# Moving part of the last split row of a ReLU row sum to ScalarE, and cutting that row's loads anew

## The chip, the cores and the metric

The kernel runs on one core of one Trainium2 chip. The metric is the device time of one execution in microseconds (us); medians over several executions are quoted. The span of a profile runs from the first to the last instruction that it shows, and in the profiles of this study the time was 1.34 to 1.35 us longer than the span. Three parts of the core matter: ScalarE (ACT in the profile), VectorE (DVE) and the sixteen DMA engines; in the page all loads and stores go through one queue (q1, 2304 packets, 67.18 MB), and SyncE (SP) issues them.

## The reference, cut to what matters

```python
x = randn(32, 512, 1024).astype(float32)          # 67 MB
out = np.sum(np.maximum(x, 0), axis=-1)           # 32 x 512 sums
```

There are 16384 rows of 1024 columns: 128 partitions with 128 rows each. Every input byte is read once, and the arithmetic is one clamp and one sum.

## The kernel before: the parts that the change and the argument touch

All loads go through one queue. Large loads of 16 rows per partition come first, then loads of 8 and 4 rows. This is the end of the stream (cuts marked, some arguments put in words):

```python
PIECES = [360, 260, 404]
...
    def act_row(ap, m, loaded):          # ScalarE: clamp and sum in one ACTIVATE
        i = nc.scalar.activation(out=ap, in_=ap, func=RELU, accum_out=res[:, m : m + 1])
        ...
    def dve_row(ap, accum_out, loaded):  # VectorE: the same in one tensor_scalar
        ...
    first = PIECES[0]
    loaded = load(..., two rows and the first 360 columns of the third)
    act_row(buf[:, c, :], m, loaded)
    dve_row(buf[:, c + 1, :], res[:, m + 1 : m + 2], loaded)
    last_loaded = load(buf[:, c + 3, :], ...)            # the last row
    ... loads of 260 and 404 columns of the third row, into tiles of their own
    act_row(buf[:, c + 3, :], m + 3, last_loaded)
    ... two stores of finished sums
    dve_row(buf[:, c + 2, :first], last[:, w : w + 1], None)                   # 360
    for i in range(1, extra):
        dve_row(parts[i - 1][:, :], last[:, w + i : w + i + 1], arrived[i - 1])  # 260
    nc.vector.wait_ge(sems.dve, n_dve)
    nc.vector.tensor_scalar(out=last[:, :], in0=last[:, :], ..., op0=MAX, op1=ADD,
        accum_out=res[:, NT - 2 : NT - 1]).wait_op(arrived[-1], 16, "sem-ge")   # 404 + 2
    store(NT - 2, 2, n_act, n_dve)
```

The third of these rows is the "split row". Its partial sums are written into extra columns behind the last piece, so the last instruction adds them up with the 404 columns. It therefore waits for VectorE's own semaphore (the partial sums) and for the last load. The final store waits for both engines.

## Time and profile before

| | value |
|---|---|
| time, median of the first 3 executions | 161.29 us |
| profiled execution | 161.02 us, span 159.67 us |
| bytes read | 67.11 MB, 421 GB/s over the span |
| VectorE, ScalarE busy | 74%, 65% of the span |

These are the occupancy lines of the page. The digits are tenths of busy time in 40 slices of 4 us, and the first two rows are VectorE and ScalarE:

```profile
DVE  0000000009999499994999999999999999999986
ACT  3000059990799708996099941999339992499985
DMA  8996996996996998979969969969969969898994
```

VectorE has nothing to do for the first 35 us, and is then busy nearly all the time to the end. The DMA row is high throughout: the packets of q1 took 98.0% of the span of sixteen engines. The last slice, the only one that the change touches, is read in the prediction from the chain of waits and the timeline. In those views L140 is line 140 of the kernel (`dve_row`), L130, or L132 after the change, is `act_row`, and L219 or L226 is the last instruction. TENSOR_SCALAR_CACHE_REDUCE is VectorE's clamp and sum, ACTIVATE is ScalarE's, and behind each stands a READ_ACCUMULATOR instruction of one column (128x1; in the trace of before 188 ns on ScalarE, 82 ns on VectorE). DVEq is an instruction of VectorE's queue, here a wait for a semaphore, and "issue" is time in which the engine waited for nothing that the profile shows.

### The profile page before, as it was taken

The page shows a single profiled execution, that of the slowest core. Times are in us where ns is not written, and L with a number is a line of the kernel's source. Part 1 is how long each engine was busy: PE and PEld are TensorE (multiplying, and loading weights), DVE is VectorE, ACT ScalarE, POOL GpSimd, SP SyncE. Part 2 cuts the span into 40 slices and gives each one's busy share as a digit, 9 for nine tenths or more (in the row PEclk, how much of TensorE's full clock was granted, in tenths as well). Part 3 has the DMA queues.
Part 4 walks back from the last instruction along what each step waited for, and adds up shares of the span by engine and source line. Part 5 has one row for each costly group of instructions (what it writes and reads, how often), then busy time and mean ns, then how long its engine had stood idle before and what let it go on. Part 6 is the DMA issues. An engine that isn't in the chain of part 4 may idle for free.

```text
span 159.7 us, 118 instructions
## 1 busy us (share of the span) xinstructions
DVE 117.5 (74%) x41; ACT 104.2 (65%) x50; POOL 0.2 (0%) x4
## 2 busy tenths in 40 slices
DVE  0000000009999499994999999999999999999986
ACT  3000059990799708996099941999339992499985
POOL 0000000000000000000000000000000000000000
DMA  8996996996996998979969969969969969898994
GB/s 279 509 525 263 525 525 263 525 525 263 525 493 296 525 410 378 525 345 443 525 263 525 525 263 525 525 263 525 525 263 525 525 263 525 345 443 386 409 408 126
DMA packets 2305, 67.18 MB, mean 421 GB/s; under 512 B 641, under 2 KB 897, under 8 KB 1025
## 3 DMA queue, kind: packets, MB, share of 16 engines
q1 hardware_dynamic: 2304, 67.18, 98.0%
q14 instruction: 1, 0.00, 0.0%
HBM read 67.11 MB, written 0.07 MB: 421 GB/s over the span
## 4 chain that ended last, share of the span: by engine, by line
DMA 43%; DVE 34%; ACT 17%; another core or an unknown queue 3%; SPq 1%; issue 0%; DVEq 0%
DMA io<-in_x_dram 43%; DVE res L123 32%; ACT io L115 17%; DVE io L140 1%; SPq L97 1%; DVE piece L219 0%; DVE piece L140 0%; DVEq L218 0%
## 5 line engine op out<-in xcount | busy, mean ns | idle before, releaser
L123 DVE TENSOR_REDUCE res<-io 128x8 f32<-128x8192 f32 (+2 forms) x9 | 101.1, 11287 | 39.9 <-ACT io L115 39.9
L115 ACT ACTIVATE io<-io 128x8192 f32<-128x8192 f32 (+2 forms) x9 | 81.7, 9110 | 47.6 <-DMA io<-in_x_dram 47.6
L130 ACT ACTIVATE io<-io 128x1024 f32<-128x1024 f32 x20 | 20.9, 1045 | 5.9 <-DMA io<-in_x_dram 5.7
L140 DVE TENSOR_SCALAR_CACHE_REDUCE io<-io 128x1024 f32<-128x1024 f32 (+1 forms) x14 | 15.5, 1165 | 0.7 <-DMA io<-in_x_dram 0.6
L130 ACT ACTIVATION_READ_ACCUMULATOR io<-io 128x1 f32 x20 | 3.8, 188 | 0.0
L115 ACT ACT_TABLE_LOAD x1 | 1.3, 1283 | 0.1
L140 DVE DVE_READ_ACCUMULATOR io<-io 128x1 f32 x14 | 1.1, 82 | 0.0
L219 DVE TENSOR_SCALAR_CACHE_REDUCE piece<-piece 128x406 f32<-128x406 f32 x1 | 0.6, 576 | 0.1
L140 DVE TENSOR_SCALAR_CACHE_REDUCE piece<-piece 128x260 f32<-128x260 f32 x1 | 0.4, 424 | 0.0
L264 POOL MEMSET const-bfloat16-1.0<- 128x1 bf16 x1 | 0.1, 101 | 0.0
L264 POOL MEMSET const-uint8-127<- 128x1 uint8 x1 | 0.1, 101 | 0.0
L264 POOL MEMSET const-float32-0.0<- 128x1 f32 x1 | 0.1, 98 | 0.2 <-issue 0.2
L264 POOL MEMSET const-float32-1.0<- 128x1 f32 x1 | 0.1, 98 | 0.0
L140 DVE DVE_READ_ACCUMULATOR piece<-piece 128x1 f32 x1 | 0.1, 83 | 0.0
L219 DVE DVE_READ_ACCUMULATOR piece<-piece 128x1 f32 x1 | 0.1, 83 | 0.0
## 6 DMA issues: line engine op xcount, KB each, us to landing
io<-in_x_dram SPq DMA_DIRECT2D x1, 4096.0 KB, 21.6
io<-in_x_dram SPq DMA_DIRECT2D x1, 2048.0 KB, 26.1
io<-in_x_dram SPq DMA_DIRECT2D x1, 1204.0 KB, 28.6
io<-in_x_dram SPq DMA_DIRECT2D x1, 512.0 KB, 29.4
piece<-in_x_dram SPq DMA_DIRECT2D x1, 202.0 KB, 29.3
piece<-in_x_dram SPq DMA_DIRECT2D x1, 130.0 KB, 29.3
io<-in_x_dram SPq DMA_DIRECT2D x7, 26.9
out_dram<-res SPq DMA_DIRECT2D x1, 55.0 KB, 1.6
```

Of the source, the lines that this page charges most:

```text
L97: dma = nc.sync.dma_start(out=dst, in_=src)
L115: i = nc.scalar.activation(out=ap, in_=ap, func=RELU)
L123: nc.vector.tensor_reduce(out=res[:, m : m + n], in_=ap, axis=mybir.AxisListType.X, op=ADD).wait_op(sems.act, n_act, "sem-ge").then_inc(se ...
L130: i = nc.scalar.activation(out=ap, in_=ap, func=RELU, accum_out=res[:, m : m + 1])
L140: i = nc.vector.tensor_scalar(out=ap, in0=ap, scalar1=0.0, scalar2=None, op0=MAX, op1=ADD, accum_out=accum_out,)
L219: nc.vector.tensor_scalar(out=last[:, :], in0=last[:, :], scalar1=0.0, scalar2=None, op0=MAX, op1=ADD, accum_out=res[:, NT - 2 : NT - 1],) ...
L264: nc = _bacc.Bacc("TRN2", target_bir_lowering=False, num_devices=1)
```

## The change

The intent: after the last byte has landed, VectorE should have less left to do. ScalarE, which ended 0.36 us before VectorE, takes the first 340 columns of the split row. The row's last 240 columns come with the last row in one load, because the two are contiguous in memory. The middle comes in loads of 220 and 224 columns, so that the last instruction has 227 columns (with three partial sums) instead of 406. The core of the diff, with cuts marked:

```diff
-PIECES = [360, 260, 404]
+ACT_PIECE, END_PIECE = 340, 240
+PIECES = [220, 224]
...
+    b = split + ACT_PIECE
+    end = split + D - END_PIECE
...
+    loaded = load(flat[:, at : at + b], src[:, :b])
+    act_row(buf[:, c, :], res[:, m : m + 1], loaded)
+    sums_act = n_act
+    act_row(flat[:, at + split : at + b], others[0], None)
+    piece_act = n_act
     dve_row(buf[:, c + 1, :], res[:, m + 1 : m + 2], loaded)
-    last_loaded = load(buf[:, c + 3, :], rows(m + 3, 1)[:, 0, :])
+    sums_dve = n_dve
+    loaded = load(flat[:, at + end : at + 4 * D], src[:, end:])
+    act_row(buf[:, c + 3, :], res[:, m + 3 : m + 4], loaded)
+    dve_row(flat[:, at + end : at + 3 * D], others[1], loaded)
...
+    for i in range(len(PIECES) - 1):
+        dve_row(parts[i][:, :], others[2 + i], arrived[i])
+    nc.vector.wait_ge(sems.act, piece_act)
     nc.vector.wait_ge(sems.dve, n_dve)
```

More of the change, by code (lines that the diff above doesn't have):

```diff
@@ L51, in __init__ @@
     def __init__(self, tc: tile.TileContext):
-        n = len(TWO) + len(TAIL) + 1 + len(PIECES)
+        n = len(TWO) + len(TAIL) + 2 + len(PIECES)
         self.loads = [tc.alloc_semaphore(f"load{i}") for i in range(n)]
@@ L64, in relu_sum @@
     assert N == P * NT == P * ROWS * (NB + 1)
-    assert sum(TAIL) == ROWS - 4 and sum(PIECES) == D
+    assert sum(TAIL) == ROWS - 4 and ACT_PIECE + END_PIECE + sum(PIECES) == D
     bufs = [nc.alloc_sbuf_tensor(f"io{i}", [P, ROWS, D], F32) for i in range(NBUF)]
     res = nc.alloc_sbuf_tensor("res", [P, NT], F32)
-    extra = len(PIECES) - 1
+    extra = len(PIECES) + 1
     parts = [
-        nc.alloc_sbuf_tensor(f"piece{i + 1}", [P, w + extra * (i + 1 == extra)], F32)
-        for i, w in enumerate(PIECES[1:])
+        nc.alloc_sbuf_tensor(f"piece{i}", [P, w + extra * (i + 1 == len(PIECES))], F32)
+        for i, w in enumerate(PIECES)
     ]
@@ L126, in total, with act_row @@
         n_dve += 1
-    def act_row(ap, m, loaded):
+    def act_row(ap, accum_out, loaded):
         nonlocal n_act
-        i = nc.scalar.activation(
-            out=ap, in_=ap, func=RELU, accum_out=res[:, m : m + 1]
-        )
+        i = nc.scalar.activation(out=ap, in_=ap, func=RELU, accum_out=accum_out)
         if loaded is not None:
@@ L166, in relu_sum @@
         for _ in range(ACT[j]):
-            act_row(buf[:, c, :], m + c, act_waits)
+            act_row(buf[:, c, :], res[:, m + c : m + c + 1], act_waits)
             act_waits = None
@@ L186, in relu_sum @@
             if i % 2 == 0 or (n == 8 and i == 7):
-                act_row(buf[:, c, :], m, loaded if i == 0 else None)
+                act_row(buf[:, c, :], res[:, m : m + 1], loaded if i == 0 else None)
             else:
@@ L191, in relu_sum @@
             m += 1
-    first = PIECES[0]
-    loaded = load(
-        buf[:, :, :].rearrange("p c d -> p (c d)")[:, c * D : (c + 2) * D + first],
-        rows(m, 3).rearrange("p c d -> p (c d)")[:, : 2 * D + first],
-    )
-    act_row(buf[:, c, :], m, loaded)
+    flat = buf[:, :, :].rearrange("p c d -> p (c d)")
+    src = rows(m, 4).rearrange("p c d -> p (c d)")
+    at = c * D
+    split = 2 * D
+    b = split + ACT_PIECE
+    end = split + D - END_PIECE
+    last, w = parts[-1], PIECES[-1]
+    others = [last[:, w + i : w + i + 1] for i in range(extra)]
+    loaded = load(flat[:, at : at + b], src[:, :b])
[3 more added lines that the diff above has]
+    piece_act = n_act
     dve_row(buf[:, c + 1, :], res[:, m + 1 : m + 2], loaded)
-    last_loaded = load(buf[:, c + 3, :], rows(m + 3, 1)[:, 0, :])
+    sums_dve = n_dve
+    loaded = load(flat[:, at + end : at + 4 * D], src[:, end:])
+    act_row(buf[:, c + 3, :], res[:, m + 3 : m + 4], loaded)
+    dve_row(flat[:, at + end : at + 3 * D], others[1], loaded)
     arrived = []
-    col = first
-    for part, w in zip(parts, PIECES[1:]):
-        arrived.append(load(part[:, :w], rows(m + 2, 1)[:, 0, col : col + w]))
-        col += w
-    sums_done = n_act, n_dve
-    act_row(buf[:, c + 3, :], m + 3, last_loaded)
-    store(0, ROWS, *freed[0])
-    store(ROWS, NT - ROWS - 2, *sums_done)
-    last, w = parts[-1], PIECES[-1]
-    dve_row(buf[:, c + 2, :first], last[:, w : w + 1], None)
-    for i in range(1, extra):
-        dve_row(parts[i - 1][:, :], last[:, w + i : w + i + 1], arrived[i - 1])
+    for part, n in zip(parts, PIECES):
+        arrived.append(load(part[:, :n], src[:, b : b + n]))
+        b += n
+    assert b == end
+    store(0, ROWS, *freed[0])
+    store(ROWS, NT - ROWS - 2, sums_act, sums_dve)
+    for i in range(len(PIECES) - 1):
+        dve_row(parts[i][:, :], others[2 + i], arrived[i])
+    nc.vector.wait_ge(sems.act, piece_act)
     nc.vector.wait_ge(sems.dve, n_dve)
```

## The prediction

> **What bounds the kernel now.** The kernel streams 67 MB through the core, so I read the load view first. The line of transfer rates on the page shows 525 GB/s peaks with 263 dips (each slice catches one or two landings of 64 KB packets) and 421 GB/s over the span; from 128 us on the loads are back to back. Nothing before 155 us is touched by the change: the same loads, rows and instructions stand there. So the whole question lies in the last five microseconds, and the next view is the chain of work that ended last, in order of time (start, length, what):
>
> ```profile
> 126.81 28.57 DMA io<-in_x_dram
> 155.39 0.02 issue
> 155.41 1.68 DVE io L140 x4
> 157.09 0.43 DVE piece L140 x2
> 157.51 0.03 issue
> 157.54 0.02 DVEq L218
> 157.56 0.07 issue
> 157.63 0.58 DVE piece L219 x2
> ```
>
> The reader is to see that the chain leaves the transfers at 155.39 us, where the load of two rows plus 360 columns lands, and is VectorE's alone from there to 158.21. The later loads land under it. The timeline of the same stretch shows both engines:
>
> ```profile
> 155.41 1.06 ACT L130 ACTIVATE io<-io 128x1024 f32<-128x1024 f32 x1 [0.45 <-DMA io<-in_x_dram]
> 155.41 1.22 DVE L140 TENSOR_SCALAR_CACHE_REDUCE io<-io 128x1024 f32<-128x1024 f32 x1 [0.57 <-DMA io<-in_x_dram]
> 156.37 0.19 ACT L130 ACTIVATION_READ_ACCUMULATOR io<-io 128x1 f32 x1
> ...
> 156.56 0.52 DVE L140 TENSOR_SCALAR_CACHE_REDUCE io<-io 128x360 f32<-128x360 f32 x1
> ...
> 156.71 1.06 ACT L130 ACTIVATE io<-io 128x1024 f32<-128x1024 f32 x1
> ...
> 157.07 0.42 DVE L140 TENSOR_SCALAR_CACHE_REDUCE piece<-piece 128x260 f32<-128x260 f32 x1
> ...
> 157.63 0.58 DVE L219 TENSOR_SCALAR_CACHE_REDUCE piece<-piece 128x406 f32<-128x406 f32 x1
> 157.67 0.18 ACT L130 ACTIVATION_READ_ACCUMULATOR io<-io 128x1 f32 x1
> ```
>
> ScalarE is idle about 0.15 us before its last row and done at 157.85, 0.36 us before VectorE. The trace's landing records (the last of the sixteen of each load) give 155.39 for the two rows and 360 columns, 156.68 for the last row, 157.05 for the 260 columns and 157.56 for the 404. So VectorE reaches each piece within 0.1 us of its landing: the end is tuned so that VectorE's chain and the last landing meet at about 157.56. After VectorE's 158.21 only the last store is left, 1.46 us to the end of the span at 159.67.
>
> [...] 1024 columns take 1042 ns, which is 189 + 853, and the next ACTIVATE starts about 0.1 us into the accumulator read. [...] 1214, 576, 424 ns for 1024, 406, 260 columns lie on 155 ns + 1.034 ns per column. [...] the trace ran at 424 in the stretch from 153 to 154 us[...]. [...] the trace shows 0.45 to 0.48 us between the end of a load's last packet and its landing, about the same for each of the four last loads.
>
> **The change part by part.**
>
> Transfers. Each load is 128 packets, eight per DMA engine one behind another. Median packets of 9632, 4096, 1616 and 1040 bytes took 369, 161, 68 and 47 ns, so about 0.0375 ns per byte between the large ones. The first load loses 20 columns (80 bytes a packet): 8 x 3 ns = 0.024 us, landing at 155.39 - 0.02 = 155.37. The second is now 1264 columns, a packet of 5056 bytes: 161 + 960 x 0.0375 = 197 ns, times 8 = 1.58 us, so it lands at about 156.94; in the kernel before, the last row alone landed at 156.68. The 220 and 224 columns are 880 and 896 bytes, about 41 and 42 ns a packet, 0.33 us each: 157.27 and 157.60. The last byte therefore lands where it did (157.56), give or take 0.04: no bytes and no packets are added or removed.
>
> ScalarE. Its row starts at 155.38. The row's accumulator read starts 0.96 us later and the next ACTIVATE about 0.09 behind that, so the added piece runs from 156.44: 189 + 340 x 0.833 = 472 ns, its accumulator read from about 156.81 to 157.00. ScalarE is free for the next ACTIVATE at about 156.90, just before the second load lands, so the last row starts at about 156.97 (0.26 us later than before), and its accumulator read ends 1.15 us later, at 158.12 rather than 157.85. The piece's sum is in place at 157.00, long before VectorE's last instruction needs it. The added 0.47 us is hidden; it fills what was ScalarE's idle time plus the later landing.
>
> VectorE. Removed: 360 columns (0.52), 260 (0.42) and 406 (0.58). Added: 240 columns (155 + 248 = 403 ns), 220 (383) and 227, 224 columns and three partial sums (390). That is 1.52 us less 1.18: 0.34 us of work gone. But the 360 columns could begin as soon as the row was done, because they came in the same load; the 240 columns come with the last row. VectorE ends its row and can start again at 155.38 + 1.15 = 156.53, and must then wait for the second load: about 0.43 us of new idle time, until 156.97. The chain from there: the next one starts 0.39 later, 157.36 (the 220 columns landed at 157.27); it and its accumulator read end at 157.75; the wait on VectorE's own semaphore and the start of the last instruction take what they take now, from 157.50 to 157.63, so 0.12 us; last instruction from 157.87 to 158.26. The extra wait on ScalarE's semaphore stands in VectorE's queue and is satisfied at 157.00; I count nothing for it.
>
> The sum. VectorE 158.26 against 158.21, ScalarE 158.12, last landing 157.60. The last store waits for both engines and costs the same 1.46 us. Net: -0.34 us of work, +0.43 us of waiting less the 0.02 us of the earlier first landing, and roundings: **+0.05 us**. On 161.29 that is 161.34 us.
>
> **The rivals.** First: the intended gain arrives. The last landing leaves only 224 columns instead of 404 behind it, 0.19 us less, and if the end really hung on the last landing, the time would be 161.1. For it: landing and VectorE's chain meet within 0.1 us now, so the kernel is nearly bound by landing. Against it: after the change the last landing at 157.60 comes before VectorE reaches it at 157.87, so the shorter last instruction is paid by a later start. It would need the second load to land about 0.25 us earlier than I work out, which is faster than the queue has ever moved those bytes. Second: ScalarE becomes the bound. It now ends 0.14 us before VectorE rather than 0.36. If the added piece with its accumulator read cost 0.2 us more than the formula, the last row would slip and the store would wait for ScalarE; about +0.1 us, 161.4. The twenty rows of one regular spacing (1.04 us) speak against such a surprise. Third: the small loads suffer. Packets of 880 and 896 bytes pay the fixed part on fewer bytes, and the second load now starts within a row; if this cost 5 ns a packet on three loads, it would be 0.12 us, about half of it before the second landing and so on the path: 161.4 to 161.45. The trace's packets of 1040 bytes, still near the line of the larger ones, speak against more.
>
> **Range and chances.** All rivals lie between 161.1 and 161.5, and the three runs before spread from 161.23 to 161.38, so another 0.1 us is for runs and chips. I take 161.34, with 161.10 to 161.60 as the range for 8 in 10. Two per cent would be 3.2 us, more than the whole time from the first changed landing to the last instruction of either engine; same has 0.98, and 0.01 stands on each side for a mishap in the runs.
>
> **What would show each step.** In the changed kernel's timeline: both engines start a row at about 155.37; ScalarE a 128x340 ACTIVATE of about 0.47 us at 156.44; VectorE then idle about 0.4 us with the transfer into the row buffer named as releaser, and its 128x240 instruction and ScalarE's last row starting together at about 156.97. If they start before 156.8, the load came faster than the queue's rate and the first rival wins. The chain of waits should leave the transfers at the second load's landing, one step later than now, and then be VectorE's through 240, 220 and 227 columns. If it ends in ScalarE's accumulator read, the second rival holds; if VectorE stands idle before the 220 or the 227 columns for a transfer, the third. The prediction is wrong as a whole if something before 155 us differs, which the order of instructions gives no reason for.

Cut from the text above, where marked, are what it quoted from outside this case and the conclusion that a load cannot land much sooner, which rested on a rate limit that was not shown here. 0.34 us of work gone, 0.43 us of waiting added and 0.02 us for the earlier first landing make +0.07 us, roundings brought it to +0.05, and on 161.29 that is 161.34. What stays of the cut paragraph is from the trace of before: the first figures are ScalarE's, and their 0.833 ns per column is what its ACTIVATEs of 7168 and 8192 columns show (6168 and 7021 ns in the mean), with 189 ns as the rest of the 1042; the line of 155 ns + 1.034 ns per column is VectorE's; the 424 is GB/s. The second load landing 0.25 us earlier would be 647 KB in 1.32 us, an estimate of 490 GB/s; the largest packets of that trace, 65536 bytes in 2418 ns (median), make 434 GB/s on sixteen engines. The "fixed part" of a packet is an estimate too: 1040 bytes took 47 ns, where 0.0375 ns per byte makes 39.

## The result, and the profile after

The changed kernel took 161.07 us (median of 6 executions, 160.93 to 161.25), the kernel before 161.22 us beside it (median of 6, 161.16 to 161.38). The ratio is 0.9990 with a 95% interval of 0.9977 to 1.0003, so no difference is shown. The measured median lies 0.03 us below the predicted range, and on the other side of the kernel before than predicted.

The chain of waits of the changed kernel, its last part (start, length, what):

```profile
127.39 29.59 DMA io<-in_x_dram
156.98 0.02 issue
157.01 0.41 DVE io L140 x2
157.42 0.32 DVE piece L140 x2
157.73 0.03 issue
157.76 0.05 DVEq L225
157.81 0.07 issue
157.88 0.40 DVE piece L226 x2
```

The chain now leaves the transfers at 156.98, at the second of the last four loads, and no longer at 155.39, at the first. From there it is VectorE's through 240, 220 and 227 columns. Its timeline (start, length, engine, line, operation; in brackets the idle time before it and what ended it):

```profile
155.42 1.06 ACT L132 ACTIVATE io<-io 128x1024 f32<-128x1024 f32 x1 [0.38 <-DMA io<-in_x_dram]
155.42 1.22 DVE L140 TENSOR_SCALAR_CACHE_REDUCE io<-io 128x1024 f32<-128x1024 f32 x1 [0.51 <-DMA io<-in_x_dram]
...
156.47 0.47 ACT L132 ACTIVATE io<-io 128x340 f32<-128x340 f32 x1
...
157.00 1.06 ACT L132 ACTIVATE io<-io 128x1024 f32<-128x1024 f32 x1
157.01 0.40 DVE L140 TENSOR_SCALAR_CACHE_REDUCE io<-io 128x240 f32<-128x240 f32 x1 [0.36 <-DMA io<-in_x_dram]
157.33 0.08 DVE L140 DVE_READ_ACCUMULATOR io<-io 128x1 f32 x1
157.33 0.38 DVE L140 TENSOR_SCALAR_CACHE_REDUCE piece<-piece 128x220 f32<-128x220 f32 x1
157.64 0.09 DVE L140 DVE_READ_ACCUMULATOR piece<-piece 128x1 f32 x1
157.88 0.39 DVE L226 TENSOR_SCALAR_CACHE_REDUCE piece<-piece 128x227 f32<-128x227 f32 x1 [0.16 <-DVE piece L140]
157.97 0.19 ACT L132 ACTIVATION_READ_ACCUMULATOR io<-io 128x1 f32 x1
```

Between its row and the 240 columns VectorE stands idle for 0.36 us, and the releaser is the transfer into the row buffer. The last instruction is released by VectorE's own earlier piece; the last load had landed at 157.57, 0.31 us before it started. ScalarE ends at 158.16 and VectorE at 158.28. The starts and ends are those that the prediction drew, to within 0.05 us. In the two profiled executions the span grew from 159.67 to 159.73 us. What went wrong lies mostly outside the picture: in the time that it was set on.

### The profile page after: what moved, and what is told of

The parts are those of the page before. It is cut to its first block, busy times and chain, and to the rows that moved or that the text cites. A ratio compares the mean times of both kernels' runs of the same rounds, so it can differ in the third digit from the quotient of the medians.

```text
span 159.7 us, 120 instructions
## 1 busy us (share of the span) xinstructions
DVE 117.2 (73%) x41; ACT 104.7 (66%) x52; POOL 0.2 (0%) x4
## 4 chain that ended last, share of the span: by engine, by line
DMA 44%; DVE 33%; ACT 17%; another core or an unknown queue 3%; SPq 1%; issue 0%; DVEq 0%
DMA io<-in_x_dram 44%; DVE res L125 32%; ACT io L117 17%; SPq L99 1%; DVE io L140 0%; DVE piece L226 0%; DVE piece L140 0%; DVEq L225 0%
## 5 line engine op out<-in xcount | busy, mean ns | idle before, releaser
L132 ACT ACTIVATE io<-io 128x1024 f32<-128x1024 f32 (+1 forms) x21 | 21.3, 1017 | 5.7 <-DMA io<-in_x_dram 5.7
```

## The experiments

Two theories of the end were tested first. **Theory C**: the end hangs on the landing of the load that carries the last row, and on VectorE's chain behind it. **Theory L**: the end hangs on the landing of the very last load. A second question was the 0.15 us between the medians: noise (**theory N**), or something that the one trace of before did not show (called theory L in the first four expectations below, since there the last landing might come late in most executions). All kernels in this section gave correct results.

To compare traces I use two points from the landing records, since the time from the start scatters: "first landing" is the last of the sixteen records of the very first load (about 21.8 us), and "A" is the same for the first of the last four loads (two rows and the first columns of the split row, about 155.4 us).

### The two kernels again, unchanged

No edit. All four ran on the same chip, the first two in the same rounds.

> The kernel before, unchanged, as a control. Theory N (the 0.15 us between the medians is run-to-run noise; the one trace of before is typical): ratio 1.000, spans about 159.7, and in its trace the last landing (404 columns) again within 0.1 us of when VectorE asks for it, at about 157.56, VectorE ending at 158.21. Theory L (in most executions of the kernel before the last loads land later against the first than in the one trace, so that the end hangs on the last landing): spans about 159.85, VectorE idle before its last instruction with the transfer as releaser.

> The changed kernel again. Theory N: its ratio to before is within 0.0005 of the control's, or 0.05 us slower by the chain (ratio 1.0003). Theory L: ratio 0.9990 (0.15 us faster) again, and clear of the control.

> A further profile of the kernel before. Theory N: VectorE ends at 158.2 and starts its last instruction on its own semaphore. Theory L: ends about 158.35 and the last instruction waits for the 404 columns.

> A further profile of the changed kernel. Both theories: VectorE idle 0.36 to 0.45 us before its 240 columns, released by the second load at about 157.0, end at about 158.27; the last landing 0.2 to 0.3 us before VectorE asks for it.

Measured: the kernel before against itself 161.15 to 161.25 us (ratio 0.9994, 0.9980 to 1.0007); the changed kernel 161.21 (ratio 0.9997, 0.9984 to 1.0009). So the same program differed from itself by 0.10 us between medians, and the 0.15 us is within what repetition gives. Theory N stands so far, with one correction: the one trace of before was not typical. Its span was 159.67 us, these two show 159.86 and 159.75. In all three the last landing came 2.16 to 2.18 us after A and VectorE ended 2.82 to 2.86 us after A, so it was not the tail that differed. In the changed kernel's second look the last load landed 0.34 us before VectorE's last instruction started, a little more than the 0.2 to 0.3 expected.

### 560 columns joined to the last row

```diff
-ACT_PIECE, END_PIECE = 340, 240
-PIECES = [220, 224]
+ACT_PIECE, END_PIECE = 340, 560
+PIECES = [62, 62]
```

> The changed kernel with 560 columns instead of 240 joined to the last row, and the two loads behind of 62 and 62. Theory C (the end hangs on the landing of the load that carries the last row, and on VectorE's chain behind it): that load lands 0.38 us later, VectorE's three pieces take 0.72 + 0.21 + 0.22 us, VectorE ends 3.26 us after the landing of the two rows and 340 columns, where it is 2.87 in the changed kernel: 0.4 us slower than it (ratio to before about 1.0025). Theory L (the last landing sets the end): 0.17 us faster than the changed kernel, because 65 columns and not 227 stand behind it. Both: scatter between executions of about 0.3 us, all of it in the spread of the first load's landing.

Measured: 161.58 us, ratio 1.0028 (1.0012 to 1.0043), slower than before with the whole interval above 1. VectorE ended 3.30 us after A (expected 3.26), against 2.88 in the changed kernel. Its timeline:

```profile
157.50 0.73 DVE L140 TENSOR_SCALAR_CACHE_REDUCE io<-io 128x560 f32<-128x560 f32 x1 [0.78 <-DMA io<-in_x_dram]
157.50 1.06 ACT L132 ACTIVATE io<-io 128x1024 f32<-128x1024 f32 x1 [0.39 <-DMA io<-in_x_dram]
158.16 0.21 DVE L140 TENSOR_SCALAR_CACHE_REDUCE piece<-piece 128x62 f32<-128x62 f32 x1
158.54 0.22 DVE L226 TENSOR_SCALAR_CACHE_REDUCE piece<-piece 128x65 f32<-128x65 f32 x1 [0.16 <-DVE piece L140]
```

The last instruction has shrunk to 0.22 us, which theory L should have rewarded with 0.17 us. Instead VectorE stands idle for 0.78 us before the joined columns, and everything behind them is later. Theory L is refuted for this form of the kernel.

### The middle in loads of 60 and 384

```diff
-PIECES = [220, 224]
+PIECES = [60, 384]
```

> The changed kernel with the middle in loads of 60 and 384 instead of 220 and 224. Theory C: VectorE's work behind the last row's load is the same, so it ends 2.88 us after the first changed landing, within 0.03 us of the changed kernel. Theory L: 160 more columns stand behind the last landing, 0.165 us slower.

Measured: 161.28 us, ratio 1.0012 (0.9998 to 1.0026), which by itself decides nothing. In the trace VectorE ended 2.94 us after A, 0.06 above the changed kernel's 2.88: more than the 0.03 that theory C allowed, and not the 0.165 of theory L.

```profile
157.21 0.40 DVE L140 TENSOR_SCALAR_CACHE_REDUCE io<-io 128x240 f32<-128x240 f32 x1 [0.42 <-DMA io<-in_x_dram]
157.54 0.21 DVE L140 TENSOR_SCALAR_CACHE_REDUCE piece<-piece 128x60 f32<-128x60 f32 x1
157.92 0.56 DVE L226 TENSOR_SCALAR_CACHE_REDUCE piece<-piece 128x387 f32<-128x387 f32 x1 [0.16 <-DVE piece L140]
```

The 387 columns are again released by VectorE's own piece, not by their load. The 0.06 us comes from the joined load, which landed 1.65 us after A here and 1.58 in the first trace of the changed kernel. So it lies in theory C's own term, and may be the scatter of one landing (1.57 to 1.63 in the six traces of the changed kernel); I claim no more than that theory L's 0.165 us did not appear.

### The new loads without ScalarE's part

```diff
     act_row(buf[:, c, :], res[:, m : m + 1], loaded)
     sums_act = n_act
-    act_row(flat[:, at + split : at + b], others[0], None)
     piece_act = n_act
     dve_row(buf[:, c + 1, :], res[:, m + 1 : m + 2], loaded)
     sums_dve = n_dve
+    dve_row(flat[:, at + split : at + b], others[0], None)
```

> The change without ScalarE's part: VectorE sums the first 340 columns, the rest as in the changed kernel. Theory C: the 340 columns (0.50 us) fill VectorE's wait of 0.36 to 0.4 us, the 240 columns start 0.05 us later than in the changed kernel, and VectorE ends 2.92 us after the first changed landing; 0.05 us slower than the changed kernel, with no idle time before the 240 columns. That is, ScalarE's part by itself takes away 0.5 us of VectorE's work and gives 0.05. A rival that holds VectorE's work to be what counts says 0.48 us slower.

Measured: 161.12 us, ratio 0.9999 (0.9986 to 1.0013). VectorE ended 2.90 us after A (expected 2.92).

```profile
156.73 0.50 DVE L140 TENSOR_SCALAR_CACHE_REDUCE io<-io 128x340 f32<-128x340 f32 x1
157.19 0.40 DVE L140 TENSOR_SCALAR_CACHE_REDUCE io<-io 128x240 f32<-128x240 f32 x1
157.19 1.06 ACT L132 ACTIVATE io<-io 128x1024 f32<-128x1024 f32 x1 [0.46 <-DMA io<-in_x_dram]
158.06 0.39 DVE L226 TENSOR_SCALAR_CACHE_REDUCE piece<-piece 128x227 f32<-128x227 f32 x1 [0.16 <-DVE piece L140]
```

This is the plainest statement of where the gain went. VectorE has 0.50 us more to do than in the changed kernel and ends 0.02 us later, because the 340 columns lie exactly in the time in which it would otherwise wait for the second load. Taking them to ScalarE turned work into waiting. The rival that counts VectorE's work asked for 0.48 us.

### A version meant to beat both

ScalarE takes 200 columns, VectorE 260 from the same load, the last row comes alone, and 220 and 344 columns follow.

```diff
-ACT_PIECE, END_PIECE = 340, 240
-PIECES = [220, 224]
+ACT_PIECE, DVE_PIECE, END_PIECE = 200, 260, 0
+PIECES = [220, 344]
...
+    dve_row(flat[:, at + a : at + b], others[1], None)
...
-    dve_row(flat[:, at + end : at + 3 * D], others[1], loaded)
```

> A version meant to beat both: ScalarE takes 200 columns and VectorE 260 from the first load, the last row comes alone, then loads of 220 and 344. Theory C: the first load lands 0.12 us later for its 100 more columns, VectorE never waits, both engines end 2.57 us after it, 0.16 us earlier than the changed kernel when both are counted from the start, 0.11 earlier than before (ratio 0.9993, below what the timing resolves; the traces, counted from the first load's last landing, resolve 0.05). Theory L: 344 columns behind the last landing, 0.06 us faster than before, 0.12 slower than the changed kernel.

> The version with 200 columns on ScalarE and 260 on VectorE once more. Counted from the first load's last landing VectorE ends at 136.39 (before 136.43 to 136.52, changed 136.42 to 136.48): at most 0.1 us ahead; ratio 0.9990 to 1.0005.

Measured: 161.22 us, ratio 1.0004 (0.9992 to 1.0017), and in the second call 161.02 us, ratio 0.9992 (0.9979 to 1.0004). By time it is not told apart from either kernel. In its two traces VectorE ended 2.69 us after A, not 2.57: the 2.57 in my expectation came from subtracting the 0.12 us of the later A from a sum that was already counted from A. Counted from the first landing it ended at 136.39 and 136.41 us, where the kernel before ended at 136.43 to 136.52 and the changed kernel at 136.42 to 136.49: 0.02 to 0.12 us earlier than either, and 0.06 on the average of before. In its second trace the profile names a transfer as the releaser of the last instruction:

```profile
156.68 0.42 DVE L140 TENSOR_SCALAR_CACHE_REDUCE io<-io 128x260 f32<-128x260 f32 x1
157.13 0.38 DVE L140 TENSOR_SCALAR_CACHE_REDUCE piece<-piece 128x220 f32<-128x220 f32 x1
157.68 0.52 DVE L227 TENSOR_SCALAR_CACHE_REDUCE piece<-piece 128x347 f32<-128x347 f32 x1 [0.16 <-DMA piece<-in_x_dram]
```

The name says less than it seems to: the last load landed at 157.54, and VectorE's own piece was done at 157.52. The last instruction started 0.16 us after that piece, as in all traces of the changed kernel, where the landing was long past. So VectorE's chain and the loads only meet again.

### The first load's 20 columns, alone

```diff
-PIECES = [360, 260, 404]
+PIECES = [340, 280, 404]
```

This is an edit of the kernel before. As a third size, `[368, 252, 404]` was tried.

> The kernel before with the 360 columns of the first of the last loads cut to 340, as in the change, and the 260 made 280; nothing else. Theory S (the first load's packets of 9552 bytes take 9 to 11 ns less than those of 9632, three times what 80 bytes should cost, and that hides the change's 0.05 us): packet median 360 ns, that load lands 133.57 us after the very first load instead of 133.61 to 133.66, VectorE ends 2.83 us behind it as before: 0.06 us earlier than before, counted from the first load. Theory R (the shift is scatter or comes with the joined load): 133.61 or later, packets 366 ns or more. Timed: ratio 0.9996 under S, not resolved.

> The kernel before with 368 and 252 columns for 360 and 260. If packets of 9632 bytes lie off the line through 9552 (360 ns) and 10032 (378 ns) for their size alone, these of 9664 bytes take 364 ns and the load lands earlier than with 9632; if the line steps up between 9552 and 9632, they take 370 or more.

The question here is a term of the prediction that looked too small: A landed 133.56 to 133.59 us after the first landing in every trace of the changed kernel, and 133.61 to 133.66 in every trace of before, 0.06 us apart on the average (133.58 and 133.63), where I had 0.024. Measured with 340 columns in the kernel before: 133.56 us, and a packet median of 360 ns, so in this one trace the shift comes with the size of that load and not with the joined load. Time 161.17 us, ratio 0.9998 (0.9985 to 1.0012), nothing resolved, as expected. VectorE ended 2.86 us after A, not 2.83, so 136.42 from the first landing against 136.46 on the average of before: 0.04, not 0.06. With 368 columns: packet median 368 ns, between the two values that I had set against each other, A at 133.68 us, 161.09 us in one execution. Looking at means rather than medians, the eight packets of an engine took 361 ns each at 9552 bytes, 368 at 9632 (364.5 in one of five traces) and 368 at 9664. That is 7 ns for 80 bytes where the large-packet slope gives 3, and 8 x 7 ns = 0.056 us agrees with the shift of A. Why these two sizes cost the additional 4 ns is open.

### More repetitions, for the 0.15 us

No edit. After the first of these five runs, 39 executions of before and 17 of the changed kernel differed by 0.08 us in the mean, with a standard error of 0.03, although the traces showed no difference; the other four runs were to show whether that stays.

> The changed kernel once more, for the pooled comparison. From the traces so far, counted from the landing of the first load, it ends 0.00 to 0.05 us earlier than before; the scatter of one execution is 0.13 us, so the ratio should be 0.9990 to 1.0005, with no sign that repeats.

> Scatter theory: from the first load's last landing to the end 137.93 us (137.88 to 137.98) whatever that landing's time; median within 0.05 us of the kernel before of the same call. If the 0.08 us is real and at the end: 137.98 or more, as the executions profiled so far would have been the quick ones.

> Scatter theory: from the first load's last landing to the end 137.92 us (137.88 to 137.96); the pooled difference to before shrinks towards 0.01 to 0.05 us. If real: stays 0.08 or more, ratio 0.9995 or less.

> As the first of this call: 137.93 us from the first landing under the scatter theory.

> As the second of this call: 137.92 us from the first landing under the scatter theory, and its first load's landing in the range 21.67 to 22.05 that all traces had so far.

Measured: the changed kernel 161.10 us, ratio 0.9996 (0.9984 to 1.0009); then, in the last call, before 161.15 and 161.26 (ratios 1.0001 and 1.0002), changed 161.25 and 161.22 (1.0000 and 0.9998), beside 161.20 for the nine executions of before in that call. Over all, the mean is 161.215 us for 58 executions of before and 161.161 for 27 of the changed kernel: 0.054 us apart, and by the scatter of 0.11 us of one execution the standard error of that difference is 0.026. The medians are 161.20 and 161.18. The difference shrank when executions were added, as the scatter theory said, though not quite to the 0.01 to 0.05 us expected. Six executions of each kernel in these pools are those that raised the question; without them the means differ by 0.029 us with a standard error of 0.029. Compared so that no chips are mixed, the 0.054 is 0.053. In the traces the expected lead of the changed kernel of up to 0.05 us did not appear either: from the first landing to the end its last three took 137.94 to 137.95 us, the last two of before 137.90 and 137.92.

What the traces say, all eleven of the two kernels (us; "spread" is between the first and the last of the sixteen landing records of the first load):

| trace | first landing | spread | A after it | VectorE's end after A | span after first landing | span |
|---|---|---|---|---|---|---|
| before | 21.76 | 0.47 | 133.63 | 2.83 | 137.92 | 159.67 |
| before | 21.97 | 0.70 | 133.61 | 2.82 | 137.89 | 159.86 |
| before | 21.78 | 0.52 | 133.66 | 2.86 | 137.97 | 159.75 |
| before | 21.87 | 0.68 | 133.61 | 2.82 | 137.90 | 159.77 |
| before | 22.01 | 0.66 | 133.66 | 2.81 | 137.92 | 159.94 |
| changed | 21.84 | 0.51 | 133.56 | 2.88 | 137.90 | 159.73 |
| changed | 22.05 | 0.80 | 133.56 | 2.87 | 137.89 | 159.94 |
| changed | 21.80 | 0.43 | 133.59 | 2.88 | 137.94 | 159.74 |
| changed | 21.67 | 0.38 | 133.57 | 2.92 | 137.95 | 159.62 |
| changed | 21.91 | 0.56 | 133.58 | 2.89 | 137.94 | 159.85 |
| changed | 22.05 | 0.67 | 133.58 | 2.90 | 137.94 | 159.98 |

Read down the columns. From the first landing to the end both kernels take the same time, 137.92 and 137.93 on average, within 0.05 us of it in every trace. The span's whole scatter of 0.36 us is in the first landing, which ranges over 0.38 us and lies 130 us before anything that the change touches. It goes with the spread of the sixteen landing records, 0.38 to 0.80 us, which stays through the stream and is at most 0.11 us less at the last load in the eleven traces: in the changed kernel's trace with the widest spread, 0.80 us, the last load's records are still 0.76 us apart, and the last record stands alone, 0.25 us behind the one before it, after the first load as after the last. That it is the same engine is inferred from this; the records don't name the engine. The traces show sixteen records for each load, and the waiting instruction starts 0.02 to 0.03 us after the last. So the end of each execution goes with the latest record of the first load and, if the inference holds, with one late engine. What makes an engine late at the start was not tested.

## Why the prediction was wrong, point by point

- **Baseline: this is the step that failed.** The prediction says "On 161.29 that is 161.34 us" and, for the scatter, "another 0.1 us is for runs and chips". 161.29 was the median of three executions, all of them above 161.20, which is the median of 58 executions of the same program; these run from 161.00 to 161.67. The profile that I read came from an execution of 161.02 us, which was in front of me and 0.2 us below all three; I took the picture from the fast execution and the base from the slow ones, and put the range around the base. With 161.20 as base and the same sum it would have been 161.25, and the measured 161.07, a median of six that happened to lie low (27 executions of the changed kernel have 161.18), would have been inside a range of the same width. The miss of 0.27 us is thus 0.09 of base, 0.05 of predicted growth that did not come, 0.02 between the pooled medians, and 0.11 by which the six executions happened to lie low.
- **First changed load: mis-sized.** "8 x 3 ns = 0.024 us" measured 0.06 us (133.63 to 133.58 after the first landing). In the one trace of the trial with 340 columns alone the load's size did it.
- **Second load: right.** 156.94 less 155.37 is 1.57 us after A; measured 1.57 to 1.63. The 220 and 224 columns were put at 1.90 and 2.23, and landed at 1.86 to 1.91 and 2.14 to 2.17; the last one came 0.06 to 0.09 us earlier than I had it. Of the times from a load's last packet to its landing the shortest is 0.44 us, not 0.45 (0.44 to 0.48 in the trace of before, for loads of 130 KB to 1.2 MB).
- **ScalarE: right.** The 340 columns took 0.47 us from 156.47 (predicted 0.472 from 156.44), the last row started at 157.00 with VectorE's piece, and ScalarE ended 2.74 to 2.80 us after A (predicted 2.75). The added piece lies in time that ScalarE had free.
- **VectorE: right in its end, partly by luck.** Work of 0.34 us gone, a wait of 0.36 us in its place, shown by the bracket in the timeline. The prediction had 0.43, counted from when VectorE could take an instruction and not from the end of its accumulator read. Its end came 2.87 to 2.92 us after A, predicted 2.89; before it was 2.81 to 2.86. But two steps inside were mis-sized and nearly cancelled. From the start of the 240 columns to that of the next piece I had 0.39 us; it took 0.33 in all six traces, because the next instruction starts 0.07 us before the one in front is shown as ended. For the wait on the semaphores and the start of the last instruction I had 0.12 us and nothing for the added wait on ScalarE's; it took 0.16 in all six traces, against 0.13 in the five of before. The chains show where: the queue's wait instruction (DVEq) took 0.05 us for two semaphores and 0.02 for one.
- **The sum: right in the tail, cancelled by the mis-sized term.** The prediction's "+0.05 us" is a tail longer by 0.07 (2.82 to 2.89 us after A) with A earlier by 0.02; its list of terms adds up to 0.07, and what it calls roundings is 0.02. The tail grew by 0.06 us (2.83 to 2.89 on average). A came 0.06 us earlier. Together: nothing.
- **Rivals.** The first, the gain arrives, is refuted by the changed kernel's own timeline, in which the last load landed 0.31 us before the last instruction started, and by the trial with 560 columns: with a last instruction of only 65 columns VectorE ended 0.42 us later. The second, ScalarE becomes the bound, did not occur: it ended 0.12 us before VectorE. The third, the small loads suffer, did not occur either: packets of 880 and 896 bytes took 41 ns, as worked out.
- **Open.** Whether the remaining 0.054 us between the pooled means (0.029 without the first six of each) is anything; no trace shows a place for it. And why packets of 9632 and 9664 bytes took 4 ns more than their bytes ask.

## What to carry to other kernels

Before work is taken off an engine at the end of a stream, ask what the engine will do in the time gained: if its next piece arrives in a later load, the work turns into a wait, as it did here (0.34 us of work gone, 0.36 us of idle time in its place), and a larger load in front of the critical piece made the wait longer (0.36 us with 240 columns joined, 0.78 with 560). When a profile and a set of timed executions are put together, check that the profiled execution is a typical one, and compare traces from a common landmark (here the first load's landing) when the expected change is smaller than the scatter of the start. Here a change of 0.1 us in 161 could be read from such traces, which from that landmark agreed within 0.05 us of their average, while six timed executions, with a scatter of 0.11 us of one, could not decide it.
